# A two-layer mixer block: compact operands for a blockwise inversion, one bank per chunk for its transitions, and another bank for the recurrence's gates

## The chip, the cores and the metric

The kernel runs on one core of a Trainium2 chip. The metric is the device time of one execution in microseconds (us), from launch to the last output written. A core has five engines with one in-order instruction queue each: PE (TensorE, matmuls, with its weight loads listed apart as PEld), DVE (VectorE), ACT (ScalarE), POOL (GpSimd) and SP (SyncE, which here only issues DMAs).

## The reference

Two layers. In each, 2048 tokens and 256 context tokens, 1024 wide, are normalised, projected by `w_in`, sent through four mixers of width 256 (a gated linear recurrence, a gated delta rule "gdn", a retention, a windowed attention), projected by `w_out` and added back. The part that the change touches most is the delta rule: for every chunk of 64 tokens, head and direction it inverts a unit lower triangular 64x64 matrix by doubling and makes chunk transitions from the inverse.

```python
def unit_lower_inverse(l_mat):
    eye = jnp.eye(l_mat.shape[-1], dtype=l_mat.dtype)
    n = -l_mat
    p = eye + n
    for _ in range(GDN_INV_STEPS):
        n = n @ n
        p = p @ (eye + n)
    return p
...
    t_mat = unit_lower_inverse(l_mat)
    u_val = t_mat @ (vs * bs[..., None])
    w_dec = t_mat @ (kb * jnp.exp(gcum)[..., None])
...
        v_new = u_i - jnp.einsum('bhcd,bhde->bhce', w_i, s)
        s_new = s * gt_i[..., None, None] + jnp.einsum('bhcd,bhce->bhde', kt_i, v_new)
```

The recurrence's gates are `sigmoid` of two 64x64-block products of its input per direction (`rglru_dir`).

## The kernel before

The sequence of 2304 tokens is 18 tiles of 128 tokens (`NT`), or 9 blocks of 256 (`NB`). A layer runs in four stages. Stage A norms each block, projects the recurrence's input and the delta rule's q, k, v (`dense_feat`, `dense_tok`), convolves them (`conv_block`) and makes the recurrence's gates and forward scan (`lru_block`). Stage B projects retention and gates per tile (dense matmuls of 512 columns into the PSUM tiles `pd`), runs retention (`ret_tile`) and the delta rule (`gdn_tile`, four worker streams `work(w)`), and the backward scan (`lru_back`). Stage C is attention and the outputs of retention and delta rule, stage D the output projection.

One tile of the delta rule holds 2 chunks, 4 heads and 2 directions, so 16 matrices of 64x64: on the partitions the two chunks (0 to 63 and 64 to 127), on the free axis 8 pairs `u` of direction and head. `gdn_tile` takes the matrix T apart into two f16 parts Ah and Al (L1016, L1017), and inverts it in levels: a masked start (L1025) and its transpose (L1027), then for k = 1 to 5 a product p1 = Ah Y (mask on DVE, L1034), a product p2 = YT M (copied by ACT, L1047), and a new transpose of Y on DVE (L1051; at k = 5 a product p3 copied by ACT, L1049, takes its place). A residual with Al and one correction (L1054 to L1073) end it. In all this `Ah` and `YT` stand as block diagonals of 128x64 by 2 (`[128, 8, 2, 64]`, zeros off the diagonal set by `memset`), so that a product over `u` is one 128x128 by 64 matmul. Every write to such an operand is two instructions, one per chunk's half of the partitions (`diag`). Two inversions can be under way at a time (`self.inv` starts as `[0, 1]`; each has the PSUM tile `pg0` or `pg1`).

Then W = T^-1 [k, v] is made (two halves, L1093), and the chunk's transition: for each chunk c and direction d a product of a 64x64 quadrant of the array, with 128 columns into banks `pm0`, `pm1` and with 64 columns into halves of the score tile `sc`. Before, the bank is c XOR d, so a bank holds chunk 0 of one direction and chunk 1 of the other; the transition's rows are added (L1126), the query part is added in four pieces of 64 partitions (L1131), and four DMAs of 64 partitions store it to `MCd` (L1136). `gdn_chain` reads it back per chunk.

`lru_block` makes the gates in the PSUM tiles `pm0`, `pm1`, which the norm's transposes (`norm_block`) use in turn, and reads them by ACT with tanh (L1249).

The order of instructions on every engine is not that of the code. `Plan` takes all instructions with their dependences, ranks them by the longest chain behind each, runs a list schedule with its own cost per instruction, and adds a dependence from each instruction to the next of its engine. Any edit can therefore move instructions anywhere.

Of the kernel before, what the change touches and what calls it, by code (L numbers as in the profile page):

```python
# [67 lines left out]
           ("rqkT", 512, 2), ("ratt", 512, 1), ("rD", 512, 1), ("rlo", 256, 1)],  # L68
          [("gA00", 512, 1), ("gQ1", 512, 1), ("gR1", 1024, 1), ("gW1", 1024, 1), ("gMC1", 1024, 1)]),
    "C": ([("sqk", 384, 1), ("sks", 384, 1), ("srope", 256, 2), ("rota", 256, 1), ("rotb", 256, 1), ("sVc", 128, 2), ("sV", 128, 5),  # L70
# [54 lines left out]
class Net:  # L125
# [507 lines left out]
    def ret_streams(self, pp):  # L633

        nc, l = self.nc, self.l
        self.tiles, self.kvs, self.wb = set(), set(), []
        self.nsc = 0
        self.busy, self.inv, self.yfull, self.st2 = [0, 0], [0, 1], [0, 0], list(range(1))
# [48 lines left out]
    def pass_b(self, pp, early):  # L687
        nc = self.nc
        self.gp = pp
        self.gA = [(self.t(pp, [128, 8, 2, 64], f"gA{i}0", F16), self.t(pp, [128, 8, 64], f"gA{i}1", F16)) for i in range(2)]  # L690
        self.gfree = list(self.gA)
        self.gYT = [self.t(pp, [128, 8, 2, 64], f"gYT{i}", F16) for i in range(2)]
        NW = 4
        for Z in [a for a, _ in self.gA] + self.gYT:
            nc.gpsimd.memset(Z, 0.0)

        def work(w):
            yield 0, 20 * w
            for t in SEQ[w::NW]:
                yield from self.gdn_tile(t, w)  # L700

        def backs():
            prev = [None, None]
            for b in [0] + list(range(NB - 1, 0, -1)):
                yield from self.lru_back(b, prev, pp)

        ret, dense = early
        self.weave([self.ahead(self.gdn_chain(0, C_HALF), 0), ret] + [work(w) for w in range(NW)] + [self.ret_scan(0, R_HALF), backs(), dense], (range(2, 2 + NW), 0))
# [169 lines left out]
    def gdn_gates(self, sp):  # L878
# [31 lines left out]
        for c in range(2):  # L910
            p2 = ps[:, 512 + 144 * c:656 + 144 * c]
            self.mm(p2, C[:, 384 + 128 * c:512 + 128 * c], f(g))
            p2v = p2.rearrange("p (t u) -> p t u", u=8)
            nc.scalar.activation(gt[0:64, :, c], p2v[0:64, :, 0:4], AF.Exp)
            nc.scalar.activation(gt[64:128, :, 1 - c], p2v[64:128, :, 4:8], AF.Exp)
        yield 0.6, 2
# [10 lines left out]
    def gdn_tile(self, t, w):  # L927
# [69 lines left out]
        T = bm  # L997
# [8 lines left out]

        def diag(fn):
            for c in range(2):
                fn(slice(64 * c, 64 * c + 64), c)

        fl = lambda a: a.rearrange("p u e -> p (u e)")
        st = lambda Z, u: Z[:, u].rearrange("p a e -> p (a e)")
        yield lambda: len(self.gfree) > 0
        slot = self.gfree.pop(0)
        Ah, Al = slot
        diag(lambda r, c: nc.scalar.copy(Ah[r, :, c], T[r]))  # L1016
        diag(lambda r, c: nc.vector.tensor_tensor(Al[r], T[r], Ah[r, :, c], op=SUB))  # L1017

# [5 lines left out]
        YT = self.gYT[s]  # L1024
        diag(lambda r, c: nc.vector.tensor_tensor(YT[r, :, c], Ah[r, :, c], lev(0)[r], op=MULT))  # L1025
        Y = t8(f"gY{s}", F16)
        diag(lambda r, c: nc.vector.transpose(Y[r], YT[r, :, c]))  # L1027
        yield 0, 2.49
        for k in range(1, 6):
            p1 = p8(self.pi(s))  # L1030
            for u in range(8):
                self.mm(p1[:, u], st(Ah, u), Y[:, u])
            M = t8(f"gM{s}", F16)
            nc.vector.tensor_tensor(M, p1, lev(k), op=MULT)  # L1034
            yield 0.25, 2.12
            p2 = p8(self.pi(s))
            for u in range(8):
                self.mm(p2[:, u], st(YT, u), M[:, u])
            if k == 5 and OWN:
                nc.scalar.copy(t8(f"gY{s}", F16), p2)  # L1040
            if k == 5:
                p3 = p8(self.pi(s) if OWN else self.slot('p3'))
                for u in range(8):
                    diag(lambda r, c: self.mm(p3[r, u], M[r, u], YT[r, u, c]))
            Y = t8(f"gY{s}", F16)
            if not (k == 5 and OWN):
                nc.scalar.copy(Y, p2)  # L1047
            if k == 5:
                diag(lambda r, c: nc.scalar.copy(YT[r, :, c], p3[r]))  # L1049
            else:  # L1050
                diag(lambda r, c: nc.vector.transpose(YT[r, :, c], Y[r]))  # L1051
            yield 0.7 if k == 5 else 0.25, 2.15
        pr = self.pi(s)
        nc.tensor.matmul(pr, self.id16, self.n16[:, None].to_broadcast([128, 8, 64]), start=True, stop=False)  # L1054
        pr = p8(pr)
        for u in range(8):
            self.mm(pr[:, u], st(Ah, u), Y[:, u], False, False)
        for u in range(8):
            diag(lambda r, c: self.mm(pr[r, u], Al[r, u], Y[r, u], False, u == 7))
        self.gfree.append(slot)  # L1060
# [8 lines left out]
        for u in range(8):  # L1069
            for A in (Rh, Rl):  # L1070
                self.mm(pr2[:, u], st(YT, u), A[:, u], A is Rh, A is Rl)
        Yf = t8(f"gYf{s}")
# [42 lines left out]
        for h in range(4):  # L1115
            for c, d, r, o in quads:
                u, pm = 4 * d + h, pms[c ^ d]
                if out_on:
                    self.mm(pm[o, h].rearrange("p (a e) -> p a e", a=2), W[r, u, 0], KA8(r, u))
                else:  # L1120
                    self.mm(pm[o, h, :64], W[r, u, 0], kd[r, u])
            for c, d, r, o in quads:
                u = 4 * d + h
                self.mm(pcs[c ^ d][o, h], kd[r, u], W[r, u, 1])
        for x in range(2):
            nc.vector.tensor_tensor(MC[:, x, 0], pms[x][:, :, 0:64], GTI[:, x], op=ADD)  # L1126
            nc.scalar.copy(MC[:, x, 1], pcs[x])
            if out_on:
                for d in range(2):
                    o = slice(64 * d, 64 * d + 64)  # L1130
                    nc.vector.tensor_tensor(Q[o, :, x ^ d], pms[x][o, :, 64:128], Q[o, :, x ^ d], op=ADD)  # L1131
        yield 2.2, 1.08
        for d in range(2):
            o = slice(64 * d, 64 * d + 64)
            for x in range(2):
                self.st('M').dma_start(self.MC[2 * t + (x ^ d), o], MC[o, x].rearrange("p a h e -> p (a h e)"))  # L1136
        if out_on:
# [92 lines left out]
    def lru_block(self, b, xb, pp):  # L1230
# [11 lines left out]
        for d in range(2):  # L1242
            th = self.t(pp, [128, 2, 256], "lthr"), self.t(pp, [128, 2, 256], "lthi", bufs=2)
            for ft in range(2):
                ps = self.pm().rearrange("p (a n) -> p a n", a=2)
                for ri in range(2):
# [801 lines left out]
```

## Time and profile before

| | |
|---|---|
| median of 3 runs | 3176.56 us (3176.01 to 3179.53) |
| profiled execution, time | 3181.56 us |
| profiled execution, span of its instructions | 3179.4 us |
| PE busy (matmuls, with the tails of the pipeline) | 2943.4 us, 93% |
| PEld busy (weight loads) | 2489.9 us, 78% |
| DVE busy | 2162.5 us, 68% |
| ACT busy | 1371.2 us, 43% |
| POOL busy | 1263.0 us, 40% |
| DMA | 504.24 MB, 50% of 16 engines' span |

The span falls into layer 0 (0 to some 1560 us) and layer 1. Stage B is 440 to 960 us in layer 0 and 2010 to 2540 us in layer 1. The share of busy time is an average over stages with different limits, so the rows below look at stage B alone where that is what counts. A matmul's span ends when its last column has left the array, so matmuls that stand close behind each other overlap; how close they can stand is read from their starts. A row "x16" of the timeline merges 16 that follow each other.

### The profile page before, as it was taken

To read this page: it belongs to the slowest core of one execution; us is meant where nothing else is said; L and a number is where in the kernel's file an instruction comes from. 1 tells how busy PE (TensorE), PEld (TensorE's weight loads), DVE (VectorE), ACT (ScalarE), POOL (GpSimd) and SP (SyncE) were. 2 spreads that over 40 slices of the span, in tenths; PEclk is the share of its full clock that TensorE was granted. 3 is DMA by queue.
4 is the path that set the end of the run, shared out by engine and by line. 5 is a ranking of instruction groups with operands and counts; after the bars stand their busy time and mean duration, and the time that the engine had idled before them with its cause. 6 is when DMAs were issued, how large, how long until landed. Compare 5 with 4: busy or idle time off the path is not lost. (4 is left out here: it accounts for less than half of the span.)

```text
span 3179.4 us, 71283 instructions
## 1 busy us (share of the span) xinstructions
PE 2943.4 (93%) x28076; PEld 2489.9 (78%) x28076; DVE 2162.5 (68%) x4578; ACT 1371.2 (43%) x3002; POOL 1263.0 (40%) x1205
## 2 busy tenths in 40 slices
PE   4999889999999899989999999799999989999887
PEld 3999767777777788876779998678777768888676
DVE  4577778788985667662245778888998747667421
ACT  3456544444443344451233556444444414445211
POOL 2143345554643223233352334455555522323332
PEclk8999989999999999999999999899999999999999
DMA  7333454545557645466553434556544575445432
GB/s 271 130 145 136 143 161 134 136 125 146 137 162 228 201 141 171 128 212 241 190 172 141 159 136 151 149 151 171 138 135 135 180 219 164 163 129 168 149 119 78
DMA packets 411247, 504.24 MB, mean 159 GB/s; under 512 B 95208, under 2 KB 312712, under 8 KB 404256
## 3 DMA queue, kind: packets, MB, share of 16 engines
q1 hardware_dynamic: 410912, 499.69, 50.0%
q8 instruction: 221, 3.62, 0.5%
q14 instruction: 114, 0.93, 0.1%
HBM read 320.06 MB, written 179.50 MB: 157 GB/s over the span
## 5 line engine op out<-in xcount | busy, mean ns | idle before, releaser
L145 PE MATMUL pd<-w,h 128*128 128x512 f32 (+1 forms) x3408 | 1006.1, 417 | 38.2 <-DVE U L1567 16.1
L145 PEld LDWEIGHTS pd<-w,h 128*128 128x128 f32 x3408 | 623.3, 196 | 166.2 <-ACT U L1565 18.5
L145 PE MATMUL pd<-h,w 128*128 128x256 f32 x3360 | 579.2, 291 | 0.6 <-DVE U L479 0.5
L145 PEld LDWEIGHTS pd<-h,w 128*128 128x128 f32 x3360 | 474.7, 192 | 9.7 <-issue 4.6
L145 PE MATMUL pm<-U 128*64 128x128 f32 (+4 forms) x3536 | 320.9, 282 | 30.5 <-ACT U L1249 10.2
L330 POOL TENSOR_TENSOR U<-U,mh 128x4 f32<-128x4 f32 (+2 forms) x174 | 181.1, 1044 | 418.2 <-DVE U L329 401.9
L145 PEld LDWEIGHTS pm<-U 128*64 128x64 f32 (+2 forms) x3536 | 239.1, 146 | 76.8 <-issue 18.0
L145 PE MATMUL pg<-h,w 128*128 128x256 f32 x1680 | 295.8, 290 | 0.0
L145 PEld LDWEIGHTS pg<-h,w 128*128 128x128 f32 x1680 | 246.7, 192 | 2.3
L145 PE MATMUL pg<-w,h 128*128 128x512 f32 x816 | 227.7, 394 | 0.8 <-DVE U L1578 0.6
L1051 DVE STREAM_TRANSPOSE U<-U 64x512 f16<-64x512 f16 x288 | 202.3, 702 | 32.5 <-ACT U L1047 28.0
L145 PEld LDWEIGHTS <-U 128*128 128x128 f16 (+1 forms) x3680 | 136.4, 102 | 71.0 <-issue 51.4
L145 PE MATMUL pg<-U 128*128 128x64 f16 (+1 forms) x3680 | 175.4, 196 | 12.7 <-DVE U L1034 9.3
L145 PEld LDWEIGHTS pg<-w,h 128*128 128x128 f32 x816 | 153.7, 189 | 41.4 <-issue 4.8
L1567 DVE TENSOR_TENSOR U<-U 128x1 f32<-128x1 f32 x34 | 8.2, 240 | 242.0 <-ACT U L1565 241.9
L625 DVE SCALAR_TENSOR_TENSOR U<-U 128x256 f32<-128x256 f32 x318 | 153.1, 527 | 2.0 <-POOL U L558 1.9
L1463 ACT ACTIVATE U<-sc,U 128x640 f32<-128x640 f32 (+2 forms) x136 | 104.0, 765 | 109.3 <-DVE U L1461 96.7
L1478 ACT COPY U<-pg 128x512 f32<-128x512 f32 (+2 forms) x248 | 100.3, 436 | 90.6 <-PE pg L1477 45.6
L1460 DVE TENSOR_REDUCE U<-sc 128x1 f32<-128x640 f32 (+2 forms) x136 | 106.3, 782 | 43.6 <-PE sc L145 42.2
L1034 DVE TENSOR_TENSOR U<-pg,C 128x512 f16<-128x512 f32 x180 | 123.3, 688 | 12.7 <-PE pg L145 8.8
L1047 ACT CAST U<-pg 128x512 f16<-128x512 f32 x144 | 84.4, 587 | 106.3 <-PE pg L145 97.3
L1565 ACT ACTIVATE U<-pd 128x512 f32<-128x512 f32 x34 | 20.0, 594 | 231.7 <-PE pd L145 117.1
(297 smaller groups left out, 6095.5 us busy)
## 6 DMA issues: line engine op xcount, KB each, us to landing
hTd<-h SPq DMA_DIRECT2D x18, 2048.0 KB
h<-hTd SPq DMA_DIRECT2D x72, 512.0 KB, 5.6
h<-hTd SPq DMA_DIRECT2D x18, 2048.0 KB, 8.2
MCd<-U SPq DMA_DIRECT2D x144, 128.0 KB, 2.4
cMC<-MCd SPq DMA_DIRECT2D x140, 128.0 KB, 3.3
U<-yTd SPq DMA_DIRECT2D x34, 512.0 KB, 6.1
U<-in_w_in_dram SPq DMA_DIRECT2D x58, 256.0 KB, 4.5
hgd<-U SPq DMA_DIRECT2D x53, 256.0 KB, 2.1
```

The costliest lines, as they stand in the source:

```text
L145: self.nc.tensor.matmul(out, lhsT, rhs, start=start, stop=stop)
L330: nc.gpsimd.tensor_tensor(out, out, self.mh[:, :n], op=ALU.pow)
L625: nc.vector.scalar_tensor_tensor(z[:, i], xb[:, f, j:j + 256], cw[:, f, j:j + 1], z[:, i], op0=MULT, op1=ADD)
L1034: nc.vector.tensor_tensor(M, p1, lev(k), op=MULT)
L1047: nc.scalar.copy(Y, p2)
L1051: diag(lambda r, c: nc.vector.transpose(YT[r, :, c], Y[r]))
L1460: nc.vector.tensor_reduce(m[:, h:h + 1], pv, axis=AX.X, op=MAXO)
L1463: nc.scalar.activation(p[:, :nk], pv, AF.Exp, bias=m[:, h:h + 1], accum_out=sums[:, h:h + 1])
L1478: nc.scalar.copy(pT[:, a:a + w], pt[:, :w])
L1565: nc.scalar.activation(x1[:, 512 * k:512 * k + 512], po[k], AF.Square, accum_out=ss[:, k:k + 1])
L1567: nc.vector.tensor_tensor(rs, ss[:, 0:1], ss[:, 1:2], op=ADD)
```

## The change

Three edits. First, `Ah` and `YT` lose their zero halves (`[128, 8, 64]`); each write to them is one instruction over 128 partitions, and each 128x128 product over `u` becomes two products of 64x64 quadrants, chunk 0 on rows and columns 0 to 63, chunk 1 on 64 to 127. Eight 128x128 matmuls become sixteen 64x64 ones, in 13 such groups per tile (10 in the five levels, 1 in the residual, 2 in the correction). Second, the transition's bank is the chunk c: `pm0` takes chunk 0 of both directions, so the query part is added in two pieces of 128 partitions and the store is two DMAs of 128 partitions. Third, the gates of the recurrence go to the two banks of the score tile `sc`, both feature halves together, as long as that tile has not been taken by retention (`self.scp is None`).

```diff
-          ... ("gA10", 512, 1), ... ("gYT1", 512, 1), ("gYT0", 512, 1), ("gA00", 512, 1)
+          ... ("gA10", 256, 1), ... ("gYT1", 256, 1), ("gYT0", 256, 1), ("gA00", 256, 1)
...
-        self.nsc = 0
+        self.nsc, self.scp = 0, None
...
-        self.gA = [(self.t(pp, [128, 8, 2, 64], f"gA{i}0", F16), self.t(pp, [128, 8, 64], f"gA{i}1", F16)) for i in range(2)]
+        self.gA = [tuple(self.t(pp, [128, 8, 64], f"gA{i}{j}", F16) for j in range(2)) for i in range(2)]
-        self.gYT = [self.t(pp, [128, 8, 2, 64], f"gYT{i}", F16) for i in range(2)]
+        self.gYT = [self.t(pp, [128, 8, 64], f"gYT{i}", F16) for i in range(2)]
-        for Z in [a for a, _ in self.gA] + self.gYT:
-            nc.gpsimd.memset(Z, 0.0)
...
-            nc.scalar.activation(gt[64:128, :, 1 - c], p2v[64:128, :, 4:8], AF.Exp)
+            nc.scalar.activation(gt[64:128, :, c], p2v[64:128, :, 4:8], AF.Exp)
...
-        def diag(fn):
-            for c in range(2):
-                fn(slice(64 * c, 64 * c + 64), c)
+        def diag(out, lhsT, rhs, start=True, stop=True):
+            for u in range(8):
+                for r in (slice(0, 64), slice(64, 128)):
+                    self.mm(out[r, u], lhsT[r, u], rhs[r, u], start, stop)
...
-        diag(lambda r, c: nc.scalar.copy(Ah[r, :, c], T[r]))
-        diag(lambda r, c: nc.vector.tensor_tensor(Al[r], T[r], Ah[r, :, c], op=SUB))
+        nc.scalar.copy(Ah, T)
+        nc.vector.tensor_tensor(Al, T, Ah, op=SUB)
...
-        diag(lambda r, c: nc.vector.tensor_tensor(YT[r, :, c], Ah[r, :, c], lev(0)[r], op=MULT))
+        nc.vector.tensor_tensor(YT, Ah, lev(0), op=MULT)
-        diag(lambda r, c: nc.vector.transpose(Y[r], YT[r, :, c]))
+        nc.vector.transpose(fl(Y), fl(YT))
...
-            for u in range(8):
-                self.mm(p1[:, u], st(Ah, u), Y[:, u])
+            diag(p1, Ah, Y)
...
-            for u in range(8):
-                self.mm(p2[:, u], st(YT, u), M[:, u])
+            diag(p2, YT, M)
...
-                diag(lambda r, c: nc.scalar.copy(YT[r, :, c], p3[r]))
+                nc.scalar.copy(YT, p3)
-                diag(lambda r, c: nc.vector.transpose(YT[r, :, c], Y[r]))
+                nc.vector.transpose(fl(YT), fl(Y))
...
-                u, pm = 4 * d + h, pms[c ^ d]
+                u, pm = 4 * d + h, pms[c]
...
-                self.mm(pcs[c ^ d][o, h], kd[r, u], W[r, u, 1])
+                self.mm(pcs[c][o, h], kd[r, u], W[r, u, 1])
...
-                for d in range(2):
-                    o = slice(64 * d, 64 * d + 64)
-                    nc.vector.tensor_tensor(Q[o, :, x ^ d], pms[x][o, :, 64:128], Q[o, :, x ^ d], op=ADD)
+                nc.vector.tensor_tensor(Q[:, :, x], pms[x][:, :, 64:128], Q[:, :, x], op=ADD)
-        for d in range(2):
-            o = slice(64 * d, 64 * d + 64)
-            for x in range(2):
-                self.st('M').dma_start(self.MC[2 * t + (x ^ d), o], MC[o, x].rearrange("p a h e -> p (a h e)"))
+        for x in range(2):
+            self.st('M').dma_start(self.MC[2 * t + x], MC[:, x].rearrange("p a h e -> p (a h e)"))
...
+            wide = self.sc() if self.scp is None else None
-                ps = self.pm().rearrange("p (a n) -> p a n", a=2)
+                ps = (self.pm() if wide is None else wide[:, 512 * ft:512 * ft + 512]).rearrange("p (a n) -> p a n", a=2)
```

On DVE in stage B of layer 0, before (`U` is the big working area, `pg` the inversions' PSUM tiles, `pm` the transitions'; L1131 is the query part, L1017 is Al, L1051 a level's transpose, L1034 the mask):

```order
L1126 TENSOR_TENSOR U_87<-pm_660_11394,U_87 128x256
L1034 TENSOR_TENSOR U_87<-pg_662_11436,C_96 128x512
L1131 TENSOR_TENSOR U_87<-pm_660_11394,U_87 64x4x64 x2
L1286 COPY U_87<-U_87 128x1
L1017 TENSOR_TENSOR F_4043<-F_4043,h_196_4044 64x512 x2
L1051 STREAM_TRANSPOSE U_87<-U_87 64x8x64 x2
```

On DVE in the same stage now (L1046 is the level's transpose, L1031 the mask, L1122 and L1125 the transition's and the query part's sums):

```order
L1046 STREAM_TRANSPOSE U_87<-U_87 128x512
L834 TENSOR_TENSOR rS_13652<-rS_13652,rsk_13649 128x256
L1031 TENSOR_TENSOR U_87<-pg_663_13284,C_96 128x512
L1122 TENSOR_TENSOR U_87<-pm_659_13168,U_87 128x256
L1125 TENSOR_TENSOR U_87<-pm_659_13168,U_87 128x4x64
```

Every pair "x2" of halves has become one instruction on all partitions, and the mask of a level now follows one transpose of the other inversion, not two.

On PE in the same stage, before, the end of one inversion's product, then a tile's transition, then the start of the other inversion's product (`pg0`, `pg1`; 64x128 and 64x64 are quadrant products, 128x64 whole-array ones; LDWEIGHTS and MATMUL of the f16 products are listed apart):

```order
L145 LDWEIGHTS U_1_87
L145 MATMUL pg0_510_9041<-U_1_87 128x64
L145 MATMUL pm0_527_9274<-F_195_4043,U_1_87 64x128 x8
L145 MATMUL sc_186_3920<-U_1_87 64x64 x16
L145 LDWEIGHTS U_1_87
L145 MATMUL pg1_534_9395<-U_1_87 128x64
```

Now, at two places of the same stage, between two inversions' products, and then to the dense projection (`pd`):

```order
L145 LDWEIGHTS h0_180_4028
L145 MATMUL pg0_470_9542<-U_1_87,h0_180_4028 64x64
L145 MATMUL pm1_487_9916<-F_179_4027,U_1_87 64x128 x8
L145 LDWEIGHTS U_1_87
L145 MATMUL pg1_480_9774<-U_1_87 64x64
```

```order
L145 LDWEIGHTS U_1_87
L145 MATMUL pg1_480_9774<-U_1_87 64x64
L145 MATMUL pd_496_10112<-w0_2_88,h1_171_3905 128x512 x3
L145 MATMUL sc_170_3904<-U_1_87,F_179_4027 64x64 x16
L145 MATMUL pd_496_10112<-w1_3_89,h1_171_3905 128x512
```

Between inversion and transition the array now keeps its shape; between inversion and dense projection it changes it, where before it did not. Over the whole program such changes of shape go from 1,067 to 1,271.

## Rows read from the trace of the kernel before

**Rows 1.** Busy time of each engine in stage B of both layers.

```profile
core 0: us, PE busy (x) PEld busy (x) DVE busy (x) ACT busy (x) POOL busy (x), PEclk, DMA share, GB/s
440.00:960.00 520.00, 500.73 (x6836) 393.31 (x6839) 443.53 (x796) 234.95 (x466) 272.56 (x236) 0.98 0.52 143
2010.00:2540.00 530.00, 503.87 (x6955) 405.18 (x6954) 465.01 (x838) 248.23 (x498) 286.68 (x251) 0.97 0.54 149
```

**Rows 2.** Groups by line, DVE: count | busy us, mean ns | idle before.

```profile
L1051 DVE STREAM_TRANSPOSE U<-U 64x512 f16<-64x512 f16 x288 | 202.3, 702 | 32.5 <-ACT U L1047 28.0
L1034 DVE TENSOR_TENSOR U<-pg,C 128x512 f16<-128x512 f32 x180 | 123.3, 688 | 12.7 <-PE pg L145 8.8
L1131 DVE TENSOR_TENSOR U<-pm,U 64x256 f32<-64x256 f32 x136 | 56.7, 418 | 1.3
L1027 DVE STREAM_TRANSPOSE U<-U 64x512 f16<-64x512 f16 x72 | 50.6, 702 | 1.2
L1025 DVE TENSOR_TENSOR U<-h,C 64x512 f16<-64x512 f16 x38 | 37.1, 977 | 0.7
L1025 DVE TENSOR_TENSOR U<-U,C 64x512 f16<-64x512 f16 x34 | 30.2, 889 | 0.4
L1017 DVE TENSOR_TENSOR F<-F,h 64x512 f16<-64x512 f32 x38 | 29.9, 786 | 7.0 <-ACT h L1016 6.3
L1017 DVE TENSOR_TENSOR U<-F,U 64x512 f16<-64x512 f32 x34 | 27.4, 807 | 4.2 <-PE pg L145 2.6 <-ACT U L1016 1.0
```

**Rows 3.** Groups by line, ACT: the copies in halves, the gates' tanh.

```profile
L1249 ACT ACTIVATE U<-pm,U 128x256 f32<-128x256 f32 x144 | 64.5, 469 | 79.7 <-PE pm L145 72.1 <-DVE U L1259 5.4 <-POOL w L444 0.6
L1049 ACT CAST U<-pg 64x512 f16<-64x512 f32 x72 | 41.7, 579 | 20.6 <-PE pg L145 19.2 <-PE pm L145 1.0
L1016 ACT CAST h<-F 64x512 f16<-64x512 f32 x38 | 23.4, 617 | 9.8 <-POOL F L1004 5.6 <-PE pg L145 3.7
```

**Rows 4.** Timeline of DVE where an inversion ends: start us, us, what.

```profile
578.48 0.69 DVE L1073 SCALAR_TENSOR_TENSOR U<-pg,U 128x512 f32<-128x512 f32 x1
579.09 1.39 DVE L1025 TENSOR_TENSOR U<-U,C 64x512 f16<-64x512 f16 x2
...
640.87 0.68 DVE L1073 SCALAR_TENSOR_TENSOR U<-pg,U 128x512 f32<-128x512 f32 x1
641.46 1.39 DVE L1025 TENSOR_TENSOR U<-h,C 64x512 f16<-64x512 f16 x2
```

**Rows 5.** Timeline of PE at four f16 groups and what starts behind each.

```profile
704.76 0.41 PE L145 MATMUL pg<-U,h 128*128 128x64 f16 x8
705.00 0.48 PE L145 MATMUL pd<-w,h 128*128 128x512 f32 x1
...
566.32 0.41 PE L145 MATMUL pg<-U 128*128 128x64 f16 x8
566.66 0.73 PE L145 MATMUL pm<-U,F 64*64 64x64 f32 x17
...
2249.45 0.44 PE L145 MATMUL pg<-U 64*64 64x64 f16 x16
2249.82 0.50 PE L145 MATMUL pd<-w,h 128*128 128x512 f32 x1
...
965.90 0.42 PE L145 MATMUL pg<-U 64*64 64x64 f16 x16
966.15 0.31 PE L145 MATMUL pm<-U,F 64*64 64x64 f32 x4
```

**Rows 6.** Groups by line, PE: transition, attention's output, recurrence's gates.

```profile
L145 PE MATMUL pm<-U 128*64 128x128 f32 x1280 | 100.1, 286 | 9.8 <-ACT U L1478 7.2 <-DVE cS L1176 2.6
L145 PE MATMUL pm<-F,U 64*64 64x128 f32 x1088 | 86.2, 276 | 0.1
L145 PE MATMUL pm<-U 128*128 128x256 f32 x288 | 83.6, 391 | 10.3 <-ACT U L1249 10.2
```

**Rows 7.** DMA issues of the page: count, KB each, us to landing.

```profile
MCd<-U SPq DMA_DIRECT2D x144, 128.0 KB, 2.4
```

More of the change, by code (lines that the diff above doesn't have):

```diff
@@ L68 @@
            ("rqkT", 512, 2), ("ratt", 512, 1), ("rD", 512, 1), ("rlo", 256, 1)],
-          [("gA00", 512, 1), ("gQ1", 512, 1), ("gR1", 1024, 1), ("gW1", 1024, 1), ("gMC1", 1024, 1)]),
+          [("gA00", 256, 1), ("gQ1", 512, 1), ("gR1", 1024, 1), ("gW1", 1024, 1), ("gMC1", 1024, 1)]),
     "C": ([("sqk", 384, 1), ("sks", 384, 1), ("srope", 256, 2), ("rota", 256, 1), ("rotb", 256, 1), ("sVc", 128, 2), ("sV", 128, 5),
@@ L1005, in gdn_tile @@
         yield 1.3, 4.6
-        def diag(fn):
-            for c in range(2):
-                fn(slice(64 * c, 64 * c + 64), c)
+        def diag(out, lhsT, rhs, start=True, stop=True):
+            for u in range(8):
+                for r in (slice(0, 64), slice(64, 128)):
+                    self.mm(out[r, u], lhsT[r, u], rhs[r, u], start, stop)
         fl = lambda a: a.rearrange("p u e -> p (u e)")
-        st = lambda Z, u: Z[:, u].rearrange("p a e -> p (a e)")
         yield lambda: len(self.gfree) > 0
@@ L1042, in gdn_tile @@
                 p3 = p8(self.pi(s) if OWN else self.slot('p3'))
-                for u in range(8):
-                    diag(lambda r, c: self.mm(p3[r, u], M[r, u], YT[r, u, c]))
+                diag(p3, M, YT)
             Y = t8(f"gY{s}", F16)
@@ L1055, in gdn_tile @@
         pr = p8(pr)
+        diag(pr, Ah, Y, False, False)
         for u in range(8):
-            self.mm(pr[:, u], st(Ah, u), Y[:, u], False, False)
-        for u in range(8):
-            diag(lambda r, c: self.mm(pr[r, u], Al[r, u], Y[r, u], False, u == 7))
+            for r in (slice(0, 64), slice(64, 128)):
+                self.mm(pr[r, u], Al[r, u], Y[r, u], False, u == 7)
         self.gfree.append(slot)
@@ L1070, in gdn_tile @@
             for A in (Rh, Rl):
-                self.mm(pr2[:, u], st(YT, u), A[:, u], A is Rh, A is Rl)
+                for r in (slice(0, 64), slice(64, 128)):
+                    self.mm(pr2[r, u], YT[r, u], A[r, u], A is Rh, A is Rl)
         Yf = t8(f"gYf{s}")
```

4 rows, old and new, of the table LAY are left out of this document.

## The prediction

> **What bounds the kernel now.** The page's chain that ended last holds only the end of the program, so the stages were read one by one: first the busy time by windows, then the groups by line with their shapes, then the timeline at single places. Nearly all that changes lies in stage B of each layer. There DVE is busy for 443.5 of 520 us (85%) and 465.0 of 530 us (88%), POOL and ACT for about half [rows 1]. PE looks fuller, 500.7 of 520 us, but a matmul's span includes its way out of the array: eight f16 matmuls at 704.76 us are shown as 0.41 us, and the next matmul starts 0.24 us after the first of them [rows 5]. Its weight loads are busy for 393.3 and 405.2 us, 76% [rows 1].
>
> The Trainium skill says in "Trainium Kernel Development and Optimization", section "Performance Expectations", that the matmul row is a bad measure of how full PE is, since matmuls are pipelined, and that the weight loads' busy share is a good one. By it PE is at 76% in stage B, and the rival of a full PE below is worth less; by the matmul row alone it would be the likeliest. The trace's 0.24 us against 0.41 us agrees.
>
> What the stage waits for is seen where an inversion ends. The last DVE instruction of one (L1073) starts at 578.48 us and the first of the next in that place (L1025) at 579.09 us; that one ends with L1073 at 640.87 us, and its successor starts at 641.46 us [rows 4]. So a place is refilled 0.6 us after it came free: both places are held nearly all the time, an inversion stays some 62 us in one, and a stage is 9 inversions in a row in each of two places. What an inversion does, and what stands in the queues before its instructions, sets the stage. One level is a matmul group, a mask of 0.69 us, a matmul group, an ACT copy and two transposes of 0.70 us each [rows 2].
>
> **The inversion's operands, DVE and ACT.** Where two halves of 64 partitions become one instruction of 128 I charge the time of one half: DVE's mask of 128x512 takes 688 ns and its transpose of 64x512 702 ns [rows 2], so the columns count and not the partitions. The transposes go from 360 to 180: 180 x 0.702 = 126 us less. The masked start is 67.3 us in 72 halves, the low part 57.3 us in 72 halves [rows 2]: half of each, 34 and 29 us less. ACT gives back 36 x 0.62 for Ah and 36 x 0.58 for the last YT [rows 3], 43 us, which nothing waits long for. Bounds for a merged transpose, which the trace does not show: 0.70 us if it is like a half, 1.40 us if like two; I take 0.70, the row nearest in kind being the mask on 128 partitions.
>
> **The same, PE.** 13 groups per tile, 36 tiles: 468 groups of eight 128x128 matmuls become groups of sixteen quadrant matmuls. Eight take 0.24 us to the next start where the neighbour has the same shape, 0.34 us where it is a quadrant group: a change of shape costs 0.10 us. Sixteen quadrant matmuls of the kind added, which p3 and the Al product already are, take 0.25 us to the next start if a quadrant group follows (965.90 us), 0.37 us if a dense one does (2249.45 us) [rows 5]. So a group between quadrant work costs 0.01 us more than before, a lonely one 0.10 + 0.37 - 0.24 = 0.23 us more. The order of the two programs has 1,067 and 1,271 changes of shape: 204 more, at 0.10 to 0.12 us, 20 to 25 us; with 468 x 0.01 = 5 us that is about 30 us on PE, 15 per stage. Bounds: 5 us if the changes cost nothing where PE idles, 468 x 0.23 = 108 us if every group were lonely.
>
> In this place the Trainium skill speaks against the change: "TensorEngine Tiling (Array Packing)", section "Restrictions and Gotchas", says that different row tiles cannot access the same PSUM bank simultaneously. The new groups alternate rows 0 to 63 and 64 to 127 in one bank, so by that rule sixteen products would queue up at 8 matmuls per 0.24 us, 0.48 us a group, and PE would get 468 x 0.24 = 112 us more. The trace has this very pattern at 0.25 us, so I go by the row.
>
> **The sum for stage B.** In its place an inversion loses five transposes (3.5 us), half a masked start (0.93 us) and an ACT half (0.58 us), together 5.0 us; the split into Ah and Al lies ahead of the place. It gets 30 us / 36 = 0.8 us of PE. Net 4.2 us, and 9 in a row make 37 us per stage. That is one bound, if the queues stay as they are; the other is +15 us per stage, if PE gives the pace. I take -17 us per stage, near half of the gain: with 37 us off, weight loads of 393 + 15 = 408 us would have to fit into 483 us (84%, now 76%), so part of what DVE gives back is spent waiting behind dense matmuls that are themselves due. DVE would then be at (443.5 - 109) / 503 = 67%, with 109 us its share of the 217 us below. What is late next is PE. Two stages: -34 us.
>
> **Transitions.** The query part goes from 136 pieces of 0.418 us [rows 2] to 68, 28 us of DVE less; with the above DVE loses 126 + 34 + 29 + 28 = 217 us. It comes after the inversion, and is in the estimate above as load. On PE the products in one bank now share their rows and differ in columns, before they shared neither. Matmuls of attention's output, also two column halves on the same rows, take 100.1 / 1280 = 78 ns each, the transition's 86.2 / 1088 = 79 ns [rows 6], so I charge nothing; without the overlap the same 1088 would take twice as long, 86 us at the outside. The 144 stores become 72 of twice the size, landing after 2.4 us [rows 7]; SP has room and the chain has the whole stage, so 0, with 72 fewer issues ahead of other loads as the cover.
>
> **Gates of the recurrence.** PE's gate matmuls idle for 10.3 us, all but 0.1 of it until ACT has read a bank [rows 6]. With two banks of their own this can go: at most -10 us. Against it, the one score tile must be read by all four tanh of a direction, 4 x 0.47 us [rows 3], before the next direction's matmuls; 36 such waits of 1.9 us are 68 us at the outside, covered by the dense projection's matmuls of other blocks, which stand between. If that cover is gone at the last block of a layer, it costs 2 us each. I take 0.
>
> **Total.** The profiled execution took 3181.56 us, 2.2 us more than its span, and lies 5.0 us above the median. 3181.6 - 34 = 3147.6 us, less 5.0 is 3143 us in the terms of the median.
>
> **Rivals.** (1) The inversion's whole shortening reaches the end, since queues get shorter as well when DVE falls from 85%: 2 x 37 = 74 us, 3103 us, or a little below. For it speaks that both places are always held; against it the weight loads at 84%. (2) The array's changes of shape give the pace: PE is the engine that never catches up in stage B, DVE's time was hidden, and 30 us are added: 3207 us, slower. For it speaks PE's 96%, against it the idle quarter in its weight loads. It decides as soon as the 15 us per stage find no gap, that is where a change of shape stands in front of dense matmuls that a `pd` reader is already waiting for. (3) What is saved is given back in stage B by POOL (272.6 of 520 us) or by a new order of the same work: no change, 3177 us. Every engine has another order now, which alone can move some microseconds either way. (4) The change does not do what it says: merged instructions cost as much as two halves, or quadrant groups queue up on their bank; then PE's 30 to 112 us stand alone, 3207 to 3289 us.
>
> **Chances.** Forecast 0.63, with a range of its own from 3120 to 3165 us; rival 1 0.15, rival 2 0.11, rival 3 0.08, rival 4 0.03. So faster by over 0.2% (6.4 us, about what a measurement of this kernel can tell from none) 0.78, within it 0.08, slower 0.14. The range from 3100 to 3185 us holds the forecast, most of rival 1 and rival 3, and leaves out the far side of rival 1 and rivals 2 and 4, some 0.2.
>
> **What would show it.** Right: transposes of 128x512 at about 0.70 us, 180 of them; DVE's busy time down by some 217 us and its share in stage B near 67%; f16 quadrant groups at 0.25 to 0.37 us; both stages B shorter by about 17 us, the other stages within a few us of before; an inversion some 4 us or more shorter in its place. Wrong: stages B as long as before with DVE idle and PE's weight loads waiting at changes of shape (rival 2); stages B over 35 us shorter (rival 1); stage A longer with matmuls of `sc` waiting for L1249's successor.

## The result and the profile after

| | time, us | ratio to the kernel before, 95% interval |
|---|---|---|
| kernel before, beside it on the same chip | 3178.05 (3176.01 to 3185.68) | |
| the change, median of 4 | 3145.92 (3140.24 to 3149.42) | 0.9891, 0.9875 to 0.9907 |

The change is faster by 1.1%, some 35 us of 3180 by the ratio and 32 us by the medians (the ratios here and below are the recorded ones; quotients of the medians differ from them by up to 0.1%). The forecast was 3143 us. The profiled execution took 3140.24 us (span 3138.5 us), 41 us less than that of before. The first part of the page after, busy us of each engine, its share of the span and its instructions:

```profile
PE 2940.4 (94%) x31820; PEld 2497.3 (80%) x31820; DVE 1938.9 (62%) x4258; ACT 1334.3 (43%) x2930; POOL 1220.2 (39%) x1197
```

DVE lost 2162.5 - 1938.9 = 223.6 us of work, PE nothing to speak of. To see which stage became shorter, the span is cut at the same events in every kernel: in each layer the first store to `gcd` (the delta rule's summed gates) ends stage A, the last store to `MCd` stage B, the last store of the mixers' outputs (`yTd`) stage C. First the kernel before, stages A, B and C of layer 0, then B and C of layer 1 (the columns are named in the first row):

```profile
core 0: us, PE busy (x) PEld busy (x) DVE busy (x) ACT busy (x) POOL busy (x), PEclk, DMA share, GB/s
0.00:401.00 401.00, 344.77 (x2560) 318.98 (x2561) 266.01 (x549) 202.24 (x388) 128.22 (x144) 0.95 0.45 164
401.00:990.00 589.00, 554.83 (x7323) 435.14 (x7321) 486.81 (x896) 269.39 (x541) 305.95 (x262) 0.96 0.54 150
990.00:1431.00 441.00, 412.83 (x3551) 357.32 (x3549) 288.34 (x817) 190.62 (x522) 130.22 (x157) 0.97 0.55 175
...
1996.00:2564.00 568.00, 534.10 (x7216) 428.44 (x7214) 487.60 (x895) 262.26 (x532) 297.16 (x260) 0.96 0.56 156
2564.00:2981.00 417.00, 393.54 (x3326) 341.48 (x3322) 276.71 (x733) 180.28 (x482) 120.98 (x145) 0.98 0.52 162
```

The same five stages after the change:

```profile
0.00:392.00 392.00, 342.65 (x2577) 318.93 (x2577) 262.65 (x551) 208.88 (x392) 111.06 (x142) 0.96 0.46 169
392.00:961.00 569.00, 543.56 (x9142) 432.41 (x9142) 380.48 (x734) 243.06 (x501) 298.50 (x260) 0.98 0.53 155
961.00:1398.00 437.00, 415.04 (x3591) 358.89 (x3587) 290.74 (x816) 191.22 (x523) 129.97 (x157) 0.97 0.55 175
...
1956.00:2508.00 552.00, 523.90 (x8964) 421.24 (x8965) 364.21 (x724) 237.82 (x491) 289.00 (x254) 0.98 0.54 158
2508.00:2940.00 432.00, 412.19 (x3443) 357.77 (x3439) 281.51 (x745) 181.75 (x487) 125.06 (x148) 0.96 0.51 159
```

Stage B is shorter by 20 us in layer 0 and by 16 us in layer 1, and DVE's share in it fell from 83 and 86% to 380.48 / 569 = 67% and 66%. But C of layer 1 is 15 us longer, and A of layer 0 is 9 us shorter, A of layer 1 7 us (558 us with the stage D ahead of it, before 565). So layer 0 keeps its gain, and in layer 1 the sum of B and C is what it was. The counts of matmuls say why B of layer 1 looks shorter: the products in quadrants add 468 x 8 / 2 = 1872 to a stage B, but there are only 8964 - 7216 = 1748 more in it, and 3443 - 3326 = 117 more in C. Work has moved from B to C. In layer 0 only 53 matmuls of 9195 left B.

The column PEclk, TensorE's granted clock, changed with the stages. It is a mean of stretches at its two levels, 2.4 GHz (1.00) and 1.2 GHz (0.50). In stage B it rose from 0.96 to 0.98 in both layers, and in C of layer 1 it fell from 0.98 to 0.96. That is some 45 us at the low level in each stage B before and some 25 us after, and in C of layer 1 some 15 us before and 35 us after (the share missing to 1.00, doubled, times the stage). In C the same 768 matmuls of one group took longer, before (first row) and after:

```profile
L145 PE MATMUL pd<-h,w 128*128 128x256 f32 x768 | 119.5, 295 | 0.0
L145 PE MATMUL pd<-h,w 128*128 128x256 f32 x768 | 125.0, 301 | 0.0
```

At half its clock PE can lose at most half of such a stretch, so by this estimate up to 10 us of each stage B's gain, and up to 10 of the 15 us that C of layer 1 got, may be the clock and not the work. All of the falls in stage B, 12 before and 6 after, come behind a stretch in which PE was busy less than on its average in the stage. One of them, in layer 0 before (the columns are those of the stages):

```profile
530.00:539.00 9.00, 4.93 (x103) 4.13 (x104) 8.72 (x16) 3.92 (x10) 5.27 (x5) 1.00 0.91 234
539.00:546.00 7.00, 6.47 (x64) 4.36 (x64) 5.76 (x13) 2.67 (x6) 2.41 (x2) 0.51 0.58 148
...
538.25 0.39 PE L145 MATMUL pg<-U 128*128 128x64 f16 x8 [1.95 <-DVE U L1034]
```

PE is busy for 4.93 of the 9 us ahead; 1.95 us of its idle time goes to a mask of DVE (last row). That a faster DVE raises the clock by closing such gaps fits these rows, but no run tests it.

The groups by line that answer to [rows 2] and [rows 3]: on DVE a level's mask (L1031), its transpose (L1046), the query part (L1125), the first transpose (L1025), the masked start (L1023), Al (L1015); on ACT the copy of p2 (L1042):

```profile
L1031 DVE TENSOR_TENSOR U<-pg,C 128x512 f16<-128x512 f32 x180 | 122.0, 684 | 64.3 <-PE pg L145 63.5
L1046 DVE STREAM_TRANSPOSE U<-U 128x512 f16<-128x512 f16 x144 | 100.8, 703 | 45.8 <-ACT U L1042 45.3
L1125 DVE TENSOR_TENSOR U<-pm,U 128x256 f32<-128x256 f32 x68 | 27.7, 410 | 0.0
L1025 DVE STREAM_TRANSPOSE U<-U 128x512 f16<-128x512 f16 x36 | 25.1, 698 | 0.2
L1023 DVE TENSOR_TENSOR U<-h,C 128x512 f16<-128x512 f16 x19 | 17.4, 916 | 2.5 <-ACT h L1014 2.5
L1023 DVE TENSOR_TENSOR U<-U,C 128x512 f16<-128x512 f16 x17 | 15.3, 902 | 0.0
L1015 DVE TENSOR_TENSOR F<-F,h 128x512 f16<-128x512 f32 x19 | 13.8, 725 | 10.5 <-ACT h L1014 9.1 <-PE pg L145 1.4
L1042 ACT CAST U<-pg 128x512 f16<-128x512 f32 x144 | 84.0, 588 | 82.9 <-PE pg L145 77.9 <-DVE U L1277 2.7 <-DVE U L1069 1.7
```

A merged instruction takes the time of one half (703 against 702 ns for a transpose). The idle time tells what is late now: DVE stands idle for 64.3 us ahead of the masks, nearly all of it for PE's product; before it was 12.7 us.

PE's groups that answer to [rows 6], the transition and the recurrence's gates (256 of the 288 are now in `sc`, 32 still in `pm`):

```profile
L145 PE MATMUL pm<-F,U 64*64 64x128 f32 x1088 | 87.5, 277 | 0.0
L145 PE MATMUL sc<-U 128*128 128x256 f32 x256 | 79.0, 390 | 6.6 <-ACT U L1242 5.8 <-DVE U L1230 0.5
L145 PE MATMUL pm<-U 128*128 128x256 f32 x32 | 9.6, 407 | 4.2 <-ACT U L1242 3.6 <-DVE U L1230 0.5
```

PE's timeline at two f16 groups (start us, us), one ahead of dense matmuls, one ahead of quadrant work, answering to [rows 5]:

```profile
465.81 0.44 PE L145 MATMUL pg<-U 64*64 64x64 f16 x16
466.18 1.19 PE L145 MATMUL pd<-w,h 128*128 128x512 f32 x4
...
526.96 0.44 PE L145 MATMUL pg<-U 64*64 64x64 f16 x16
527.24 0.30 PE L145 MATMUL sc<-cS,cMC 64*64 64x64 f32 x2
```

Sixteen quadrant products take 0.37 us to the next start with a change of shape behind them, 0.28 us without.

DVE's timeline where an inversion ends (L1069) and its successor starts (L1023), answering to [rows 4]:

```profile
597.06 0.69 DVE L1069 SCALAR_TENSOR_TENSOR U<-pg,U 128x512 f32<-128x512 f32 x1 [0.59 <-PE pg L145]
597.67 0.68 DVE L1023 TENSOR_TENSOR U<-U,C 128x512 f16<-128x512 f16 x1
...
655.34 0.68 DVE L1069 SCALAR_TENSOR_TENSOR U<-pg,U 128x512 f32<-128x512 f32 x1
655.94 0.68 DVE L1031 TENSOR_TENSOR U<-pg,C 128x512 f16<-128x512 f32 x1
656.54 1.03 DVE L1023 TENSOR_TENSOR U<-h,C 128x512 f16<-128x512 f16 x1
```

This inversion stays 58.4 us, the one of [rows 4] 62.5 us.

### The profile page after: what moved, and what is told of

Its sections match the earlier page's. It is cut to its first block, busy times and chain, and to the rows that moved or that the text cites. A ratio compares the mean times of both kernels' runs of the same rounds, so it can differ in the third digit from the quotient of the medians.

```text
span 3138.5 us, 78206 instructions
## 1 busy us (share of the span) xinstructions
PE 2940.4 (94%) x31820; PEld 2497.3 (80%) x31820; DVE 1938.9 (62%) x4258; ACT 1334.3 (43%) x2930; POOL 1220.2 (39%) x1197
## 5 line engine op out<-in xcount | busy, mean ns | idle before, releaser
L145 PE MATMUL pd<-w,h 128*128 128x512 f32 (+1 forms) x3408 | 984.4, 411 | 26.2 <-DVE U L1560 16.1
L145 PEld LDWEIGHTS pd<-w,h 128*128 128x128 f32 x3408 | 613.4, 192 | 158.6 <-ACT U L1558 18.5
L145 PE MATMUL pd<-h,w 128*128 128x256 f32 x3360 | 589.2, 294 | 1.1 <-DVE U L479 1.1
L145 PE MATMUL pm<-U 128*64 128x128 f32 (+4 forms) x3280 | 249.4, 274 | 26.4 <-ACT U L1089 7.7
L145 PEld LDWEIGHTS pm<-U 128*64 128x64 f32 (+2 forms) x3280 | 197.6, 143 | 68.4 <-issue 22.3
L145 PEld LDWEIGHTS <-U 64*64 64x64 f16 x6512 | 153.2, 109 | 55.1 <-issue 45.4
L145 PE MATMUL pg<-U 64*64 64x64 f16 x6512 | 188.4, 195 | 1.2 <-DVE U L1031 1.1
L1031 DVE TENSOR_TENSOR U<-pg,C 128x512 f16<-128x512 f32 x180 | 122.0, 684 | 64.3 <-PE pg L145 63.5
L625 DVE SCALAR_TENSOR_TENSOR U<-U 128x256 f32<-128x256 f32 x318 | 159.8, 552 | 1.1 <-POOL U L558 1.1
L1046 DVE STREAM_TRANSPOSE U<-U 128x512 f16<-128x512 f16 x144 | 100.8, 703 | 45.8 <-ACT U L1042 45.3
L1042 ACT CAST U<-pg 128x512 f16<-128x512 f32 x144 | 84.0, 588 | 82.9 <-PE pg L145 77.9
```

The source lines that it names most:

```text
L145: self.nc.tensor.matmul(out, lhsT, rhs, start=start, stop=stop)
L625: nc.vector.scalar_tensor_tensor(z[:, i], xb[:, f, j:j + 256], cw[:, f, j:j + 1], z[:, i], op0=MULT, op1=ADD)
L1046: nc.vector.transpose(fl(YT), fl(Y))
```

## The experiments

Theory: the inversions' shorter DVE work, less PE's changes of shape, sets the gain, and it lies in the compact operands. Rivals: the gain is the new order of the instructions; or it comes from the transitions or the gates; or from the granted clock, which no experiment set apart.

**The compact operands, taken apart.** Four kernels. The first has the first edit alone: the hunks of the diff in `pass_b` and in `gdn_tile` down to L1073.

```diff
+        nc.scalar.copy(Ah, T)
+            diag(p1, Ah, Y)
+                nc.vector.transpose(fl(YT), fl(Y))
...
```

> Only the compact inversion operands; transitions and gates as before. If the shorter stay of an inversion in its place is the whole gain, 32 to 36 us less than before, some 3144 us against 3178. If the 17 us that stages A lost in the changed kernel come from the gates, 15 to 20 us less than before, some 3160 us, and stages A as long as before.

The second has the quadrant products, but every write to an operand stays in halves of 64 partitions:

```diff
-                nc.vector.transpose(fl(YT), fl(Y))
+                for r in halves:
+                    nc.vector.transpose(fl(YT)[r], fl(Y)[r])
```

> Compact operands and quadrant products, but every DVE and ACT write to them in two halves of 64 partitions as before; transitions and gates as before. It adds to the kernel before only what the quadrant products cost on PE. By the prediction's term 30 us more, some 3208 us, stages B 15 us longer each. If quadrant products slip into quadrants that a transition leaves free, so that they cost nothing, 3178 us within 6 us.

The third is the other half: the kernel before with its 128x128 products, where each write is one instruction on all partitions, into one column block of the old operands.

```diff
-        diag(lambda r, c: nc.scalar.copy(Ah[r, :, c], T[r]))
+        nc.scalar.mul(Ah[:, :, 0], T, 0.25)
...
-                diag(lambda r, c: nc.vector.transpose(YT[r, :, c], Y[r]))
+                nc.vector.transpose(YT[:, :, 0], Y)
```

> Whole-array products of block operands as before, but each write to such an operand is one instruction over 128 partitions into one block column (so the two chunks are mixed, Ah is scaled by 0.25 to stay finite, and the output isn't the reference's); transitions and gates as before. It has the merged writes without the quadrant products. By the prediction's terms 34 + 30 us less, some 3114 us. If the quadrant products cost PE nothing, about the time of the kernel with only compact operands, 3145 to 3160 us.

The fourth has the third edit alone:

```diff
+            wide = self.sc() if self.scp is None else None
-                ps = self.pm().rearrange("p (a n) -> p a n", a=2)
+                ps = (self.pm() if wide is None else wide[:, 512 * ft:512 * ft + 512]).rearrange("p (a n) -> p a n", a=2)
```

> Only the recurrence's gates in the two banks of the score tile. By the prediction 0, 3178 us within 6 us. If the 17 us that stages A lost in the changed kernel come from it, some 3161 us with both stages A 8 to 9 us shorter. If the single score tile makes directions wait for each other at the end of a layer, 4 to 12 us more than before.

Measured, against 3182.91 us for the kernel before in these rounds:

| | median us | ratio, 95% interval |
|---|---|---|
| compact operands alone | 3160.95 | 0.9925, 0.991 to 0.994 |
| quadrant products, writes in halves | 3207.88 | 1.0078, 1.0062 to 1.0095 |
| whole-array products, merged writes | 3137.02 | 0.9852, 0.9837 to 0.9868 |
| gates alone | 3181.93 | 0.9994, 0.9983 to 1.0004 |

The two halves can each be read twice. Quadrant products cost 3207.88 - 3182.91 = 25 us, and 3160.95 - 3137.02 = 24 us where the writes are merged. Merged writes give 3207.88 - 3160.95 = 47 us, and 3182.91 - 3137.02 = 46 us with whole-array products. (With four kernels, that the pairs agree is one check and not two.) Net, the operands give 22 us. Each kernel here stands for one order of its instructions, and an order alone moved the kernel before by up to 22 us (below): the writes are clear of that, the price of the products hardly.

The kernel with halves met its expectation (3208 us). The compact operands alone gave less than the 32 to 36 us expected if the shorter stay were the whole gain. The merged writes came out between their two expectations, 3114 and 3145 to 3160 us. The gates gave nothing, so the compact operands' 3160.95 us, though near the 3160 us expected if stage A's loss came from the gates, don't show that: stage A of layer 0 took 394 us in both kernels with compact operands, 396 with the gates alone, 400 with whole-array products and 401 before.

The windows of stage B place the two effects. Quadrant products with writes in halves, 599 and 587 us:

```profile
394.00:993.00 599.00, 559.85 (x9154) 443.69 (x9153) 490.01 (x899) 267.23 (x540) 303.64 (x260) 0.95 0.53 147
...
2007.00:2594.00 587.00, 547.69 (x9047) 436.99 (x9046) 474.68 (x885) 263.34 (x530) 295.21 (x257) 0.95 0.54 151
```

Whole-array products with merged writes, 558 and 548 us:

```profile
400.00:958.00 558.00, 531.83 (x7292) 426.19 (x7290) 393.38 (x767) 243.95 (x505) 297.86 (x262) 0.97 0.56 157
...
1966.00:2514.00 548.00, 518.99 (x7184) 414.84 (x7184) 388.96 (x764) 236.78 (x494) 290.98 (x257) 0.97 0.58 161
```

So both effects lie in stage B: +10 and +19 us for the products, -31 and -20 us for the writes, against 589 and 568 us before. DVE is busy for 490 us of the stage of layer 0 in the one and 393 us in the other. The groups of the kernel with writes in halves show the half transposes, and PE's products at the same mean as after:

```profile
L1053 DVE STREAM_TRANSPOSE U<-U 64x512 f16<-64x512 f16 x288 | 202.0, 702 | 37.5 <-ACT U L1047 32.3
L145 PE MATMUL pg<-U 64*64 64x64 f16 x6512 | 193.5, 197 | 15.3 <-DVE U L1036 11.7 <-DVE U L1030 1.4 <-ACT U L1041 1.1
```

The groups of the kernel with merged writes: here too the masks (L1034) wait for PE, for 41 us where it was 12.7 us, though no quadrant product was added. So 29 of the 52 us by which this wait grew in the change come with the merged writes alone.

```profile
L1034 DVE TENSOR_TENSOR U<-pg,C 128x512 f16<-128x512 f32 x180 | 122.4, 683 | 41.4 <-PE pg L145 39.3
L1051 DVE STREAM_TRANSPOSE U<-U 128x512 f16<-128x512 f16 x144 | 101.2, 705 | 52.4 <-ACT U L1047 51.2
```

The gates alone are worth nothing that can be measured. Their windows for stages A and B of layer 0:

```profile
0.00:396.00 396.00, 335.84 (x2527) 310.84 (x2527) 262.25 (x553) 207.42 (x386) 112.18 (x144) 0.93 0.46 166
396.00:986.00 590.00, 556.63 (x7323) 442.08 (x7325) 487.61 (x893) 268.19 (x541) 303.79 (x262) 0.96 0.54 149
986.00:1434.00 448.00, 418.07 (x3588) 361.62 (x3583) 290.80 (x817) 190.54 (x523) 130.34 (x157) 0.98 0.55 171
```

Stage A is 5 us shorter, B 1 us and C (the third row) 7 us longer: what stage A gains is given back within the layer.

**The transitions, and each pair of edits.** The second edit alone:

```diff
-                u, pm = 4 * d + h, pms[c ^ d]
+                u, pm = 4 * d + h, pms[c]
...
+                nc.vector.tensor_tensor(Q[:, :, x], pms[x][:, :, 64:128], Q[:, :, x], op=ADD)
```

> Only the bank per chunk of the transitions; inversion and gates as before. By the prediction 0, 3183 us within 6 us against 3183 before. If DVE's 28 us and 72 DMAs less are worth what is missing between compact operands alone (-22 us) and the whole change (-35 us), some 13 us less, 3170 us.

The whole change without the second edit (these hunks undone), and without the third (`self.pm()` for the gates as before):

> Compact operands and gates in the score banks; transitions with banks by c XOR d as before. If the three edits add up and the missing 13 us belong to the transitions, 3161 us. If they come from gates and compact operands together, 3148 us.

> Compact operands and transitions with a bank per chunk; gates in the pm banks as before. If the missing 13 us belong to the transitions, alone or with quadrant products that run in the array's half that a transition now leaves free, 3148 us. If they need the gates, 3161 us.

And the whole change with another order of the same instructions. `TURN` is the weight with which the list schedule avoids a change of shape when it picks PE's next group:

```diff
-TURN = 25.0
+TURN = 40.0
```

> The whole change, with the planner's weight of a change of the array's shape 40 instead of 25, which puts the same instructions in another order (1,286 changes of shape for 1,271). It measures what an order alone is worth: 3146 us within 6 us if little, 10 us or more off in either direction if the 13 us can be an accident of the order.

Measured, against 3185.32 us for the kernel before:

| | median us | ratio, 95% interval |
|---|---|---|
| transitions alone | 3166.34 | 0.9941, 0.9928 to 0.9953 |
| operands and gates | 3145.67 | 0.9878, 0.9862 to 0.9894 |
| operands and transitions | 3155.04 | 0.9904, 0.9889 to 0.9919 |
| whole change, weight 40 | 3170.16 | 0.9952, 0.9938 to 0.9966 |

The transitions alone came nearer to the 3170 us of their second expectation than to the 3183 us of no effect; operands and gates met 3148 us; operands and transitions lie between their two. In us of 3180: operands 24, transitions 19, gates 2; operands with transitions 31, with gates 39; all three 35. The parts don't add up, and leaving out the transitions loses nothing (0.9878 against 0.9891, intervals overlapping), though alone they gave 19 us. And the order alone took 0.9952 - 0.9891 = 0.6%, 19 us, from the whole change: the rival of the order is as large as the parts. The page and a group of the kernel with the transitions alone:

```profile
PE 2931.8 (93%) x28076; PEld 2487.2 (79%) x28076; DVE 2145.2 (68%) x4510; ACT 1370.6 (43%) x3002; POOL 1266.9 (40%) x1205
...
L145 PE MATMUL pm<-F,U 64*64 64x128 f32 x1088 | 92.4, 286 | 0.9 <-ACT U L984 0.4 <-ACT U L1110 0.2
L1129 DVE TENSOR_TENSOR U<-pm,U 128x256 f32<-128x256 f32 x68 | 27.9, 413 | 0.6 <-ACT U L1110 0.5
```

The query part costs 27.9 us instead of 56.7, as reckoned, and the transition's matmuls no less than before (92.4 us against 86.2): the bank as such gave PE nothing.

**Both kernels in other orders.** So the kernel before and the change were each run with the weights 20 (shown) and 30:

```diff
-TURN = 25.0
+TURN = 20.0
```

> The whole change with the planner's weight of a change of shape at 20: the same instructions in a third order. If the edits bring some 30 us whatever the order and an order scatters by 10 us, 3140 to 3165 us. If the order decides, anywhere between 3130 and 3190 us, and no better than the kernel before with the same weight.

> The kernel before with the weight at 20. If the edits bring some 30 us whatever the order, 3175 to 3195 us, 20 us or more above the changed kernel with the same weight. If the order decides, as good as that one.

> The whole change with the weight at 30: a fourth order. If the edits bring some 30 us whatever the order, 3140 to 3165 us; if the order decides, anywhere between 3130 and 3190 us.

> The kernel before with the weight at 30. If the edits bring some 30 us whatever the order, 3175 to 3195 us, 20 us or more above the changed kernel with the same weight; if the order decides, as good as that one.

Measured, against 3183.3 us for the kernel before at weight 25; the row of 25 is from the runs above:

| weight | kernel before: us, ratio, interval | the change: us, ratio, interval | difference |
|---|---|---|---|
| 20 | 3176.19, 0.9972, 0.996 to 0.9983 | 3162.34, 0.9924, 0.9911 to 0.9938 | 0.48%, 15 us |
| 25 | 1 | 3145.92, 0.9891, 0.9875 to 0.9907 | 1.09%, 35 us |
| 30 | 3198.05, 1.004, 1.0025 to 1.0054 | 3170.4, 0.9957, 0.994 to 0.9973 | 0.83%, 26 us |

The order alone moves the kernel before within a range of 0.68%, 22 us, and the change within 0.66%, 21 us. Neither expectation holds as it stands: at 20 the change is not 20 us ahead, at 30 both kernels lie above the ranges given for edits that work whatever the order, but the change never falls back to the kernel before. In all three pairs the change is faster, by 15 to 35 us, 0.8% or 25 us on average, and weight 25 happens to be the best of the change's four. So of the 35 us some 25 belong to the edits and some 10 to the luck of this order. With three pairs that split is an estimate, and parts under 20 us, the transitions alone among them, can't be told from an order.

**The clock, which no run was made for.** The profiled executions of the seven kernels that have quadrant products and merged writes both were granted 0.965 to 0.969 of TensorE's clock over the whole span, those of the seven others, with products alone (0.963) and merged writes alone (0.964) among them, 0.961 to 0.964. Executions of the kernel before differ in clock too: in the three groups of 17, 11 and 21 that stood beside the experiments, a straight line gives 1.3 to 2.7 us less time per 0.001 more. By this estimate the 0.005 between the kernel before (0.964) and the change (0.969) goes with 6 to 13 us of the 35. It would still be an effect of the edits, but through the clock and not through the queues that the prediction reckoned with. It also means that the pairs above don't all compare at one clock (the 24 us for the products are 0.969 against 0.964). Why the two halves of the edit raise it only together stays open.

## Why the prediction was right, and where not

**Stage B is set by the inversions, and DVE's merged halves shorten them: right for DVE and for layer 0.** DVE lost 224 us (217 reckoned), its share in B is 67 and 66% (67), a merged transpose takes 0.70 us (taken from between 0.70 and 1.40). With halves, the compact operands are slower than the kernel before (1.0078): rival 4's first case made by hand, with 3207 us forecast for it and 3207.88 us measured (the forecast was 30 us above the 3177 us of the kernel before, the measurement 25 us above the 3182.91 us beside it).

**PE's 30 us for quadrant products: about right in size, too small on the path.** It measured 24 to 25 us of time. But the sum took only 7.5 us of it per stage, and then near half of the net; measured it was 10 and 19 us. How much PE's own work grew was not measured apart; if it was the 30 us reckoned, most of it arrived, as rival 2 said of PE. The weight loads' share of stage B was 74 and 75% before and is 76% now, and yet the idle quarter was little room for new work. The Trainium skill, in "Trainium Kernel Development and Optimization", section "Performance Expectations", names that share, beside another, as a good metric for how close a kernel is to the roofline. Here it did not tell what work for PE would cost.

**"Near half of the gain": right in the total by two errors that cancel, so the 3 us between forecast and median are luck.** Reckoned gross, the writes were 18 x 5.0 = 90 us in the places; 47 us arrived. The operands' net was to be 34 us and is 22 to 24. The remainder came from terms that were put at 0 or left out: the transitions and gates in this order, the order itself, and perhaps the clock. The range of the forecast is sounder than its middle: at the other weights the change's ratios of 0.9924 to 0.9957 would make 3152 to 3163 us of the 3176.56 us, still within 3120 to 3165 us.

**"What is late next is PE": right; "some 4 us or more" per inversion: wrong on average.** The idle time ahead of the masks grew by 64.3 - 12.7 = 52 us, 1.4 us for each of the 36 inversions, of the 4.2 us that each was to lose. The two timelines show 4 us less for one stay, but the stage's own count is smaller: from the first start to the last end of the inversions, stage B went from 531.8 to 514.2 us in layer 0 and from 509.2 to 505.0 us in layer 1, 2.0 and 0.5 us per inversion. In layer 1 the other 12 us of the stage came off behind the last inversion, where 26 us were left to the last store to `MCd` and 14 are now.

**Two stages B of -17 us, the others within a few us: the first right, the second wrong.** B lost 20 and 16 us, but C of layer 1 got 15 us, and the two stages A lost 9 and 7 us that no term held. B and C of layer 1 together take 985 us before and 984 us after: 117 matmuls moved from B to C, and C had some 20 us more at the low clock; how the 15 us divide between the two is not shown. So the stage's -17 us was in layer 1 a shift, and rival 3 (given back by a new order) held there though not in layer 0. Rival 3 gave an order "some microseconds"; it measured up to 22. It is not this order's alone: of the five kernels at weight 25 whose stage B of layer 1 was shorter by over 10 us, four had a C longer by 11 to 15 us, the one with whole-array products by 2 us. Why layer 1 keeps less than layer 0 stays open. The removed `memset` calls were not priced either: 8 of 0.95 us on POOL, with none waiting for them.

**The transitions at 0: not confirmed.** Alone they gave 19 us, within the change nothing. Their DVE share (28 us reckoned, 28.8 measured in the query part) is real, PE's part is none, the 72 stores landed after 3.3 us instead of 2.4 with none waiting; what else made the 19 us stays open, since another order moves as much. The stores after:

```profile
MCd<-U SPq DMA_DIRECT2D x72, 256.0 KB, 3.3
```

**The gates at 0: right.** Alone 0.9994. PE's idle time ahead of the gates, at most 10 us of which was to go, did not fall at all: 10.3 us before, 6.6 + 4.2 = 10.8 us after in the two groups. Alone, stage A gained 5 us and the layer's later stages took it back. With the operands they look worth 15 us (39 less 24), a size that an order has too.

**The rivals.** Rival 1 (all 74 us arrive) fails at 35 us. The merged writes without the quadrant products gave 46 us, about half of the 90 us reckoned for them; there DVE stood idle for 29 us more ahead of the masks, nearly all for PE, and 20 us more ahead of the transposes, for ACT. Rival 2 is half true: the products cost 24 to 25 of its 30 us, but the DVE side gave more.

## What to carry to other kernels

An instruction of DVE on 128 partitions took what one on 64 did (703 and 702 ns for a transpose), so a layout that lets two halves be written at once is worth looking for, even at the price of more and smaller matmuls; take the price on PE as if little of it were hidden, though, when PE feeds the chain that sets the stage (here 24 to 25 of 30 us). Before a gain of under 1% is put down to an edit of a scheduled program, run both versions in a few other orders: here the same instructions differed by up to 0.7%. Read the granted clock beside the times: a stage can get shorter because it was granted more. And look at the stage behind the one that got shorter: work may have moved there.

## What the runs showed of the hardware

Quadrant products of an inversion start among those of a transition, before its last ones have started. PE's timeline after the change, where a transition (`pm`) is followed by an inversion's product (`pg`):

```profile
627.38 0.54 PE L145 MATMUL pm<-F,U 64*64 64x128 f32 x5
627.66 0.21 PE L145 MATMUL pg<-U,h 64*64 64x64 f16 x1
627.66 0.48 PE L145 MATMUL pm<-F,U 64*64 64x128 f32 x4
627.88 0.23 PE L145 MATMUL pg<-U,h 64*64 64x64 f16 x2
...
628.21 0.32 PE L145 MATMUL pg<-U,h 64*64 64x64 f16 x8
628.46 1.20 PE L145 MATMUL pd<-w,h 128*128 128x512 f32 x4
```

The first f16 product starts at 627.66 us while transition matmuls go on, and the dense group starts at 628.46 us, 0.25 us after the first of the last eight. That the two kinds use different halves of the array's rows at that moment is likely by the code, but the trace does not name the rows. Such overlap does not pay for the quadrant products: with the writes in halves they cost 25 us.

The Trainium skill says in "TensorEngine Tiling (Array Packing)", section "Restrictions and Gotchas", that different row tiles cannot access the same PSUM bank simultaneously. Sixteen products that alternate between the two row halves in one bank took 0.28 us to the next start, against 0.24 us for eight whole-array products [rows 5]; one after the other at the latter's pace they would take 0.48 us. So the trace shows no queue on the bank. The two row halves write different partitions of the bank here (`out[r, u]` in the diff).
